# Regrouping a split-product QKV matmul: pairs of row blocks in groups of two, and a later second half of the leftover columns

## The chip, the cores and the metric

The kernel runs on one core of a Trainium2 chip. The metric is the device time of one execution in microseconds (us). Engines are named as the profile names them: PE is TensorE (matmul), PEld its weight loads, DVE is VectorE, ACT is ScalarE, POOL is GpSimd, SP is SyncE, which issues most of the DMAs; ACTq and SPq are the DMA issues of ACT and SP.

## The reference

```python
def reference(x, w_qkv):            # x: 16 x 512 x 768, w_qkv: 768 x 2304, float32
    qkv = np.matmul(x, w_qkv)       # 8192 x 768 times 768 x 2304
    q, k, v = qkv[..., :768], qkv[..., 768:1536], qkv[..., 1536:]
    return np.stack([q, k, v], axis=0).astype(np.float32)
```

## The kernel before

The 8192 rows of x are taken as 32 **pairs** p = 0 to 31, each of two blocks of 128 rows. K = 768 is six slices of 128 (KT = 6), in two halves of three (KH = 3). Of the 2304 columns, 2048 are two **quads** (q = 0 and 1) of two blocks of 512 columns; the other 256 columns, in the middle, are the remaining columns, `REM`.

A quad of a pair is a 2 x 2 by 2 x 2 block product (row blocks by K halves, K halves by column blocks). It is computed with seven block products in place of eight, in Winograd's form. Each product is three matmuls of 128 x 128 by 128 x 512. Products 1 and 2 use rounded copies of x and w in bf16 (`xb`, `b1`). Products 3 to 7 use sums of blocks in fp32r: of x in `s` (made by `sums_x`, five operations on POOL, L211 to L215), of w in `t` (made once by `sum_w`, L120 on DVE) and in `b22`. The remaining columns are plain bf16 products: `rem`, twelve matmuls with 256 columns for a pair (L299).

The order of work is written out by hand (`manual_schedule`): each engine does its instructions in the order in which the program issues them. A pair in the steady part is `two(a, b, early)`, with a and b its quads:

1. product 1 of a and of b (bf16); ACT copies each result to the output tile `o` (`evacuate`, L253).
2. `early()`: the work ahead for pair p+1 and the loads for pair p+2. `ahead(p+1)` is `transpose` (L154, one DVE instruction), `round_x` (L191, a cast to bf16 on POOL) and `sums_x` on POOL. The load of a pair (`load_x`) is four DMAs, two from SP and two from ACT.
3. `rem(p)`, and ACT's copy of it (L316) and its store (L317).
4. product 2 of a and of b (bf16); DVE adds each to `o` (L266).
5. products 6, 6, 5, 7, 5, 7, 4, 3, 4, 3 of a and b (fp32r), with copies by ACT (L269, L275, L279) and additions by DVE (L276, L282); a quad is stored after its product 3 (`store_quad`, two DMAs on SP).

So PE changes from fp32r to bf16 and back once for each pair. The pools hold 8 PSUM banks (`ps`), 5 output tiles (`o`), 3 `xin`, 2 `xf`, 4 `xb` and 2 `s`. A single further buffer, `both`, holds at first a staged block of w and its bf16 copy `bt`, and then the output tile of quad 1 of pair 2.

Pairs 0 to 2 run while w is still being loaded. Pairs 0 and 1 are done as plain bf16 products by K slices: `block(0, 0, ...)`, the first 512 columns, and `block(0, 1, bt, ...)`, the second 512 (L472), whose w slices are cast by DVE and ACT as they land (`cast_j`, L448 and L450). Then come, in this order on PE: the remaining columns of pairs 0 and 1 (`rems_by_halves`, L327, 24 matmuls: K half 0 of both pairs, then K half 1), products 1 and 2 of the first quad of pair 2, `rem(2)`, products 5 and 6 of that quad, and so on. `w_rem[0]` and `w_rem[1]`, the two K halves of the remaining columns of w, are loaded and cast to bf16 by one DMA each from POOL's queue (L435). `hold(src)` puts a one-column copy to a tile `mark` on POOL (L430) ahead of them, so that POOL waits there until `src` has landed: here the last slice of the first 512 columns.

For pair 2, DVE turns the rows in two halves (`transpose(2, 2)`), and ACT rounds one row block at a time (`round_row`, L200). On DVE the first half stands behind `sum_w(0, 2)`, which needs the last slice of the second 512 columns.

Of the kernel before, what the change touches and what calls it, by code (L numbers as in the profile page):

```python
# [10 lines left out]
def kernel(  # L11
# [130 lines left out]
    def load_x(p, other):  # L142
        xin[p] = xin_pool.tile([P, 2 * P // G, KC], fp32, name="xin")
        load_x_half(p, 0, nc.sync)
        if other is not None:
            load_x_half(p, 1, other)

    def transpose(p, parts=1):
        t = xf_pool.tile([P, KT, 2 * P], fp32, name="xf")
        turned = t[:].rearrange("p j (g b) -> p g j b", b=G)  # L150
        rows = xin.pop(p)[:].rearrange("p g (a j) -> p g j a", a=G)
        n = 2 * P // G // parts
        for g in range(0, 2 * P // G, n):
            nc.vector.transpose(turned[:, g:g + n], rows[:, g:g + n])  # L154
        xf[p] = t

# [27 lines left out]
            [xb[p][:, n, r * P:(r + 1) * P] for n in ks], [t[:] for t in ps]  # L186
        )

    def round_x(p):
        xb[p] = xb_pool.tile([P, KT, 2 * P], bf16, name="xb", tag="xb")  # L190
        nc.gpsimd.tensor_copy(out=xb[p][:], in_=xf[p][:])  # L191

    act, dve = nc.scalar, nc.vector

    def round_row(p, r, eng):
        n = slice(r * P, (r + 1) * P)
        if r == 0:
            xb[p] = xb_pool.tile([P, KT, 2 * P], bf16, name="xb", tag="xb")
        if eng is act:
            eng.activation(xb[p][:, :, n], xf[p][:, :, n], ident)  # L200
        else:
            eng.tensor_copy(out=xb[p][:, :, n], in_=xf[p][:, :, n])

    def sums_x(p, eng=None):
        t = xf.pop(p)
        a11, a12 = t[:, :KH, :P], t[:, KH:, :P]
        a21, a22 = t[:, :KH, P:], t[:, KH:, P:]
        s = s_pool.tile([P, 5, KH, P], f32r, name="s")
        sr[p] = s
        sums = {  # L210
            1: lambda g: g.tensor_tensor(s[:, 1], a21, a22, op=add),  # L211
            2: lambda g: g.tensor_tensor(s[:, 2], s[:, 1], a11, op=sub),  # L212
            3: lambda g: g.tensor_tensor(s[:, 3], a11, a21, op=sub),  # L213
            0: lambda g: g.tensor_copy(out=s[:, 0], in_=a22),
            4: lambda g: g.tensor_tensor(s[:, 4], a12, s[:, 2], op=sub),  # L215
        }
        if eng is not None:
            return sums
        for n in (1, 2, 3, 0, 4):
            sums[n](nc.gpsimd)  # L220
# [5 lines left out]
    def quad(p, q, pool=o_pool, tag="o"):  # L226
        u = Quad()
        u.p, u.q = p, q
        u.o = pool.tile([P, 2, 2 * CB], fp32, name="o", tag=tag)
        u.x = u.y = u.z = None  # L230
        return u
# [20 lines left out]
    def evacuate(u):  # L252
        nc.scalar.activation(u.o[:, 0, :CB], u.x[:], ident)  # L253

    def do(u, n, out=True):
        c11, c12 = u.o[:, 0, :CB], u.o[:, 0, CB:]
        c21, c22 = u.o[:, 1, :CB], u.o[:, 1, CB:]
        if n == 1:
            u.x = bank()
            product(u, 1, u.x, True)  # L260
            if out:
                evacuate(u)
        elif n == 2:
            u.z = bank()
            product(u, 2, u.z, True)
            nc.vector.tensor_tensor(c11, c11, u.z[:], op=add)  # L266
        elif n == 6:
            product(u, 6, u.x, False)
            nc.scalar.activation(c12, u.x[:], ident)  # L269
        elif n == 5:  # L270
            u.y = bank()
            product(u, 5, u.y, True)
        elif n == 7:
            product(u, 7, u.x, False)
            nc.scalar.activation(c22, u.x[:], ident)  # L275
            nc.vector.tensor_tensor(c22, c22, u.y[:], op=add)  # L276
        elif n == 4:
            product(u, 4, u.x, False)
            nc.scalar.activation(c21, u.x[:], ident)  # L279
        elif n == 3:  # L280
            product(u, 3, u.y, False)
            nc.vector.tensor_tensor(c12, c12, u.y[:], op=add)  # L282
# [21 lines left out]
    def rem(p, eng=nc.sync, between=None):  # L304
        ps = ps_pool.tile([P, 2, REM], fp32, name="ps")
        rem_row(p, 0, ps[:, 0, :])
        if between is not None:
            between()
        rem_row(p, 1, ps[:, 1, :])
        return rem_copied(p, ps, eng)  # L310

    def rem_copied(p, ps, eng=nc.sync):

        def copied():
            o = or_pool.tile([P, 2, REM], fp32, name="orem")
            act.activation(o[:], ps[:], ident)  # L316
            return lambda: eng.dma_start(rows_of(1, p, R_OFF - H, R_OFF - H + REM), o[:])  # L317

        return copied

    def rems_by_halves(pairs):
        banks = [ps_pool.tile([P, 2, REM], fp32, name="ps") for _ in pairs]
        for h in range(2):
            for p, ps in zip(pairs, banks):
                for r in range(2):
                    for j in range(KH):
                        nc.tensor.matmul(  # L327
                            ps[:, r, :], xb[p][:, h * KH + j, r * P:(r + 1) * P],
                            w_rem[h][:, j, :], start=(h == 0 and r == 0 and j == 0),
                            stop=(h == 1 and j == KH - 1), skip_group_check=True,  # L330
                        )
        return [rem_copied(p, ps) for p, ps in zip(pairs, banks)]

    def two(a, b, early, u=None):

        do(a, 1)
        do(b, 1, u is None)
        if u is None:
            early()
            rem(a.p)()()  # L340
        else:
            middle(u)
            copied = rem(a.p, between=lambda: third(u))
            evacuate(b)
            early()
            copied()()
            fourth(u)
        do(a, 2)
        do(b, 2)
        do(a, 6)  # L350
        do(b, 6)
        do(a, 5)
        do(a, 7)
        do(b, 5)
        do(b, 7)
        do(a, 4)
        do(a, 3)
        store_quad(a)
        do(b, 4)
        do(b, 3)  # L360
        store_quad(b)
# [14 lines left out]
    def last(a, b):  # L376

        p = a.p

        def rem_stored(r):  # L380
            ps = bank()
            rem_row(p, r, ps[:, :REM])
            o = or_pool.tile([P, 2, REM], fp32, name="orem")
            nc.scalar.activation(o[:, 0, :], ps[:, :REM], ident)  # L384
            row = (2 * p + r) * P
            nc.scalar.dma_start(out_flat[1, row:row + P, R_OFF - H:R_OFF - H + REM], o[:, 0, :])  # L386

        do(a, 1)
        do(b, 1)
        do(a, 2)  # L390
        do(a, 6)
        do(b, 2)
        do(b, 6)
        for u in (a, b):
            store_cols(u, 0, 0, CB, nc.sync)
        for u in (a, b):
            do(u, 5)
            do(u, 7)
            store_cols(u, 1, CB, 2 * CB, nc.sync)
        do(a, 4)  # L400
        store_cols(a, 1, 0, CB, nc.scalar)
        rem_stored(0)
        do(b, 4)
        store_cols(b, 1, 0, CB, nc.scalar)
        for u in (a, b):
            do(u, 3)
            store_cols(u, 0, CB, 2 * CB, nc.sync)
        rem_stored(1)
# [19 lines left out]
    def hold(src):  # L428
        mark = m_pool.tile([P, 1], fp32, name="mark")
        nc.gpsimd.tensor_copy(out=mark[:], in_=src)  # L430

    hold(stage[0, 1, 0][:, KH - 1, :1])
    for h in range(2):
        rows = w_qkv.rearrange("(p j) n -> p j n", j=KT)[:, h * KH:(h + 1) * KH]
        nc.gpsimd.dma_start(w_rem[h][:], rows[:, :, R_OFF:R_OFF + REM])  # L435
    hold(xin[2][:, 0, :1])
# [65 lines left out]
    def ahead(p):  # L502
        transpose(p)
        round_x(p)
        sums_x(p)
# [28 lines left out]
    for f in late0:  # L534
# [5 lines left out]
    sum_w(0, 2)  # L540
    nc.gpsimd.tensor_copy(out=b22[0][:], in_=stage[0, 1, 1])
    late = block(
        0, 1, bt, [((j, ), range(4)) for j in range(KH)] + [(range(KH, KT), range(4))]
    )
    rems = rems_by_halves(range(2))
    transpose(2, 2)

    late[0]()
    late[1]()
    round_row(2, 0, act)  # L550
    rem_stores = [rems[0]()]
    late[2]()
    late[3]()
    round_row(2, 1, act)
    rem_stores.append(rems[1]())
    load_blocks(1, 1)
    for store in rem_stores:
        store()
# [7 lines left out]
    sums[2](dve)  # L566
    sum_w(0, 3)
    sums[3](dve)
    sums[4](dve)

    u = quad(2, 0)
    do(u, 1)
    do(u, 2)
    cast_j(1, 0, b1[1], 0)
    rem2 = rem(2)
    middle(u, (5, 6))
# [38 lines left out]
    do(u2, 1)  # L615
    do(u2, 2)

    for p in range(ND + 1, NP):
        def early():
            if p + 1 < NP:  # L620
                ahead(p + 1)
            if p + 2 < NP:
                load_x(p + 2, nc.sync if p <= ND + 2 else nc.scalar)

        a, b = quad(p, 0), quad(p, 1)
        if p == ND + 1:
            two(a, b, early, u2)
        elif p < NP - 1:
            two(a, b, early)
        else:  # L630
            last(a, b)


# [28 lines left out]
```

## Time and profile before

| what | value |
|---|---|
| time, median of 3 runs | 360.31 us (359.99 to 360.98) |
| the profiled execution: time | 361.83 us |
| the profiled execution: span of its instructions | 360.0 us |
| PE busy | 353.4 us (98%), 1780 matmuls |
| DVE, ACT, POOL busy | 227.8, 185.6, 178.6 us |
| granted TensorE clock | 1.0 |
| DMA | 107.73 MB, mean 299 GB/s |
| DMA share and rate, 20.5 to 55.3 us | 1.01, 344 GB/s |
| DMA share and rate, 55.3 to 345 us | 0.92, 294 GB/s |

A PE that is busy is not a PE at its peak: a matmul's record overlaps the next one's, so what counts is the distance between starts. "Idle before" in a row is the engine's idle time ahead of it, with what ended it behind the arrow.

### The profile page before, as it was taken

The page shows a single profiled execution, that of the slowest core. Times are in us where ns is not written, and L with a number is a line of the kernel's source. Part 1 is how long each engine was busy: PE and PEld are TensorE (multiplying, and loading weights), DVE is VectorE, ACT ScalarE, POOL GpSimd, SP SyncE. Part 2 cuts the span into 40 slices and gives each one's busy share as a digit, 9 for nine tenths or more (in the row PEclk, how much of TensorE's full clock was granted, in tenths as well). Part 3 has the DMA queues.
Part 4 walks back from the last instruction along what each step waited for, and adds up shares of the span by engine and source line. Part 5 has one row for each costly group of instructions (what it writes and reads, how often), then busy time and mean ns, then how long its engine had stood idle before and what let it go on. Part 6 is the DMA issues. An engine that isn't in the chain of part 4 may idle for free.

```text
span 360.0 us, 5279 instructions
## 1 busy us (share of the span) xinstructions
PE 353.4 (98%) x1780; PEld 251.2 (70%) x1780; DVE 227.8 (63%) x244; ACT 185.6 (52%) x316; POOL 178.6 (50%) x187
## 2 busy tenths in 40 slices
PE   7999999999999999999999999999999999999995
PEld 3465577777777777777777777777777777777764
DVE  2789776756566675566675566675556676556643
ACT  4469744545454545454545444455444445545443
POOL 0221676446664445664445665444665444665420
PEclk9999999999999999999999999999999999999999
DMA  7998999898998999899999899998999998989767
GB/s 271 330 356 306 332 359 394 257 321 308 275 325 300 296 275 291 280 322 301 291 283 286 284 310 308 292 283 285 288 297 315 293 294 272 296 283 322 292 238 257
DMA packets 82107, 107.73 MB, mean 299 GB/s; under 512 B 5409, under 2 KB 62241, under 8 KB 82081
## 3 DMA queue, kind: packets, MB, share of 16 engines
q1 hardware_dynamic: 66672, 96.35, 82.4%
q10 hardware_dynamic: 14608, 10.65, 8.9%
q0 software_dynamic: 800, 0.39, 0.8%
q8 instruction: 14, 0.23, 0.3%
q14 instruction: 13, 0.10, 0.1%
HBM read 32.28 MB, written 75.50 MB: 299 GB/s over the span
## 4 chain that ended last, share of the span: by engine, by line
PE 93%; DMA 5%; ACT 1%; ACTq 1%; issue 0%
PE ps L244 78%; PE ps L299 11%; PE ps L472 4%; DMA st<-in_w_qkv_dram 3%; DMA touch<-in_x_dram 1%; PE ps L327 1%; ACT o L279 0%; ACTq L370 0%; ACT orem L384 0%; ACT both L448 0%; ACTq L416 0%; ACTq L386 0%; ACTq L384 0%
## 5 line engine op out<-in xcount | busy, mean ns | idle before, releaser
L244 PE MATMUL ps<-t,s 128*128 128x512 f32 x720 | 181.1, 399 | 0.0
L244 PEld LDWEIGHTS ps<-t,s 128*128 128x128 f32 x720 | 134.9, 188 | 30.9 <-ACT o L269 0.3
L191 POOL CAST xb<-xf 128x1536 bf16<-128x1536 f32 x28 | 40.9, 1462 | 131.1 <-DVE xf L154 131.1
L276 DVE TENSOR_TENSOR o<-o,ps 128x512 f32<-128x512 f32 x58 | 39.9, 687 | 90.5 <-ACT o L275 90.5
L154 DVE STREAM_TRANSPOSE xf<-xin 128x1536 f32<-128x1536 f32 (+1 forms) x32 | 88.9, 2783 | 2.6 <-DMA xin<-in_x_dram 2.5
L244 PE MATMUL ps<-b,xb 128*128 128x512 bf16 x360 | 87.7, 380 | 0.0
L244 PEld LDWEIGHTS <-xb 128*128 128x128 bf16 x360 | 32.8, 98 | 37.3 <-issue 7.6
L269 ACT ACTIVATE o<-ps 128x512 f32<-128x512 f32 x60 | 35.9, 598 | 44.0 <-PE ps L244 41.3
L275 ACT ACTIVATE o<-ps 128x512 f32<-128x512 f32 x58 | 34.7, 598 | 44.3 <-PE ps L244 44.3
L282 DVE TENSOR_TENSOR o<-o,ps 128x512 f32<-128x512 f32 x60 | 41.2, 687 | 21.4 <-PE ps L244 20.2
L244 PE MATMUL ps<-b,s 128*128 128x512 f32 x180 | 50.4, 389 | 0.0
L253 ACT ACTIVATE o<-ps 128x512 f32<-128x512 f32 x60 | 35.8, 597 | 24.4 <-DVE o L282 20.6
L279 ACT ACTIVATE o<-ps 128x512 f32<-128x512 f32 x60 | 35.9, 598 | 24.2 <-PE ps L244 21.3
L299 PE MATMUL ps<-w_rem,xb 128*128 128x256 bf16 x360 | 44.6, 273 | 0.0
L299 PEld LDWEIGHTS <-xb 128*128 128x128 bf16 x360 | 34.9, 98 | 11.1 <-issue 1.1
L266 DVE TENSOR_TENSOR o<-o,ps 128x512 f32<-128x512 f32 x60 | 37.8, 670 | 2.0 <-ACT o L253 1.3
L244 PEld LDWEIGHTS ps<-b,s 128*128 128x128 f32 x180 | 33.8, 188 | 7.1
L212 POOL TENSOR_TENSOR s<-s,xf 128x384 fp32r<-128x384 f32 x29 | 29.4, 1014 | 2.3
L215 POOL TENSOR_TENSOR s<-xf,s 128x384 fp32r<-128x384 f32 x29 | 29.4, 1015 | 0.0
L213 POOL TENSOR_TENSOR s<-xf 128x384 fp32r<-128x384 f32 x29 | 29.4, 1013 | 0.0
L211 POOL TENSOR_TENSOR s<-xf 128x384 fp32r<-128x384 f32 x29 | 29.3, 1012 | 0.0
L316 ACT ACTIVATE orem<-ps 128x512 f32<-128x512 f32 x31 | 18.5, 597 | 20.6 <-PE ps L299 20.1
(47 smaller groups left out, 125.9 us busy)
## 6 DMA issues: line engine op xcount, KB each, us to landing
out_dram<-o SPq DMA_DIRECT2D x62, 768.0 KB, 4.9
out_dram<-o SPq DMA_DIRECT2D x65, 256.0 KB, 4.0
xin<-in_x_dram SPq DMA_DIRECT2D x62, 192.0 KB, 6.9
xin<-in_x_dram ACTq DMA_DIRECT2D x50, 192.0 KB, 4.3
out_dram<-orem SPq DMA_DIRECT2D x31, 256.0 KB, 5.9
st<-in_w_qkv_dram SPq DMA_DIRECT2D x11, 256.0 KB, 5.8
st<-in_w_qkv_dram SPq DMA_DIRECT2D x3, 768.0 KB, 8.7
xin<-in_x_dram SPq DMA_DIRECT2D x4, 384.0 KB, 5.1
```

What stands on the lines that cost most here:

```text
L154: nc.vector.transpose(turned[:, g:g + n], rows[:, g:g + n])
L191: nc.gpsimd.tensor_copy(out=xb[p][:], in_=xf[p][:])
L212: 2: lambda g: g.tensor_tensor(s[:, 2], s[:, 1], a11, op=sub),
L244: nc.tensor.matmul(ps[:], lhs[j], rhs[j], start=(start and j == 0), stop=(j == KH - 1), skip_group_check=True,)
L253: nc.scalar.activation(u.o[:, 0, :CB], u.x[:], ident)
L266: nc.vector.tensor_tensor(c11, c11, u.z[:], op=add)
L269: nc.scalar.activation(c12, u.x[:], ident)
L275: nc.scalar.activation(c22, u.x[:], ident)
L276: nc.vector.tensor_tensor(c22, c22, u.y[:], op=add)
L279: nc.scalar.activation(c21, u.x[:], ident)
L282: nc.vector.tensor_tensor(c12, c12, u.y[:], op=add)
L299: nc.tensor.matmul(ps, xb[p][:, j, r * P:(r + 1) * P], w_rem[j // KH][:, j % KH, :], start=(j == 0), stop=(j == KT - 1), skip_group_check= ...
```

## The change

Two parts of the order are changed.

**At the start.** The load of `w_rem[1]` gets a `hold` of its own: POOL now waits for the last slice of the second 512 columns before it issues this DMA. `rems_by_halves` only does K half 0 at once and hands back K half 1, which is done behind products 1 and 2 of pair 2's first quad; these move up. ACT's copies of both pairs' remaining columns, and their stores, follow K half 1. The addition of product 2 (`add_z`) is moved between the sums on DVE. In `block(0, 1, ...)` the fourth K slice is also done for all four tiles before the last two slices are done tile by tile.

**Pairs 6 to 29.** They run as twelve groups of two (`group`): products 1, `rem` and products 2 of the first pair, then the same of the second pair, then the fp32r products of the first pair and then of the second (`rounded`). One output tile of four is taken from the buffer `both`. The transposition of pair p+3 now stands on DVE between the additions of product 2 and those of the first pair's fp32r products; `sums_x` of the second pair begins at the group's start, with `round_x` after its first sum. Loads are issued one or two pairs earlier in pairs 3 to 5, and from SP except for two of the eight DMAs of a group. Pairs 3 to 5, 30 and 31 keep the order of before; pair 5 carries the transposition of pair 7 in two parts (`turns`).

```diff
@@ -145,14 +145,20 @@
         if other is not None:
             load_x_half(p, 1, other)
 
-    def transpose(p, parts=1):
+    def transpose(p, parts=1, split=False):
         t = xf_pool.tile([P, KT, 2 * P], fp32, name="xf")
         turned = t[:].rearrange("p j (g b) -> p g j b", b=G)
         rows = xin.pop(p)[:].rearrange("p g (a j) -> p g j a", a=G)
         n = 2 * P // G // parts
-        for g in range(0, 2 * P // G, n):
-            nc.vector.transpose(turned[:, g:g + n], rows[:, g:g + n])
+        turns = [
+            lambda g=g: nc.vector.transpose(turned[:, g:g + n], rows[:, g:g + n])
+            for g in range(0, 2 * P // G, n)
+        ]
         xf[p] = t
+        if split:
+            return turns
+        for turn in turns:
+            turn()
 
 
 
@@ -186,9 +192,10 @@
             [xb[p][:, n, r * P:(r + 1) * P] for n in ks], [t[:] for t in ps]
         )
 
-    def round_x(p):
+    def round_x(p, t=None):
+        t = xf[p] if t is None else t
         xb[p] = xb_pool.tile([P, KT, 2 * P], bf16, name="xb", tag="xb")
-        nc.gpsimd.tensor_copy(out=xb[p][:], in_=xf[p][:])
+        nc.gpsimd.tensor_copy(out=xb[p][:], in_=t[:])
 
     act, dve = nc.scalar, nc.vector
 
@@ -252,6 +259,10 @@
     def evacuate(u):
         nc.scalar.activation(u.o[:, 0, :CB], u.x[:], ident)
 
+    def add_z(u):
+        c11 = u.o[:, 0, :CB]
+        nc.vector.tensor_tensor(c11, c11, u.z[:], op=add)
+
     def do(u, n, out=True):
         c11, c12 = u.o[:, 0, :CB], u.o[:, 0, CB:]
         c21, c22 = u.o[:, 1, :CB], u.o[:, 1, CB:]
@@ -263,7 +274,8 @@
         elif n == 2:
             u.z = bank()
             product(u, 2, u.z, True)
-            nc.vector.tensor_tensor(c11, c11, u.z[:], op=add)
+            if out:
+                add_z(u)
         elif n == 6:
             product(u, 6, u.x, False)
             nc.scalar.activation(c12, u.x[:], ident)
@@ -320,7 +332,8 @@
 
     def rems_by_halves(pairs):
         banks = [ps_pool.tile([P, 2, REM], fp32, name="ps") for _ in pairs]
-        for h in range(2):
+
+        def half(h):
             for p, ps in zip(pairs, banks):
                 for r in range(2):
                     for j in range(KH):
@@ -329,9 +342,11 @@
                             w_rem[h][:, j, :], start=(h == 0 and r == 0 and j == 0),
                             stop=(h == 1 and j == KH - 1), skip_group_check=True,
                         )
-        return [rem_copied(p, ps) for p, ps in zip(pairs, banks)]
-
-    def two(a, b, early, u=None):
+
+        half(0)
+        return lambda: half(1), [rem_copied(p, ps) for p, ps in zip(pairs, banks)]
+
+    def two(a, b, early, u=None, turns=()):
 
         do(a, 1)
         do(b, 1, u is None)
@@ -347,12 +362,20 @@
             fourth(u)
         do(a, 2)
         do(b, 2)
+        rounded(a, b, turns)
+
+    def rounded(a, b, turns=()):
+
+        for t in turns[:1]:
+            t()
         do(a, 6)
         do(b, 6)
         do(a, 5)
         do(a, 7)
         do(b, 5)
         do(b, 7)
+        for t in turns[1:]:
+            t()
         do(a, 4)
         do(a, 3)
         store_quad(a)
@@ -429,8 +452,8 @@
         mark = m_pool.tile([P, 1], fp32, name="mark")
         nc.gpsimd.tensor_copy(out=mark[:], in_=src)
 
-    hold(stage[0, 1, 0][:, KH - 1, :1])
     for h in range(2):
+        hold(stage[0, 1, h][:, KH - 1, :1])
         rows = w_qkv.rearrange("(p j) n -> p j n", j=KT)[:, h * KH:(h + 1) * KH]
         nc.gpsimd.dma_start(w_rem[h][:], rows[:, :, R_OFF:R_OFF + REM])
     hold(xin[2][:, 0, :1])
@@ -540,19 +563,23 @@
     sum_w(0, 2)
     nc.gpsimd.tensor_copy(out=b22[0][:], in_=stage[0, 1, 1])
     late = block(
-        0, 1, bt, [((j, ), range(4)) for j in range(KH)] + [(range(KH, KT), range(4))]
+        0, 1, bt,
+        [((j, ), range(4)) for j in range(KH + 1)] + [(range(KH + 1, KT), range(4))],
     )
-    rems = rems_by_halves(range(2))
+    second_half, rems = rems_by_halves(range(2))
     transpose(2, 2)
 
     late[0]()
     late[1]()
     round_row(2, 0, act)
-    rem_stores = [rems[0]()]
     late[2]()
     late[3]()
+    u = quad(2, 0)
+    do(u, 1)
+    do(u, 2, False)
     round_row(2, 1, act)
-    rem_stores.append(rems[1]())
+    second_half()
+    rem_stores = [r() for r in rems]
     load_blocks(1, 1)
     for store in rem_stores:
         store()
@@ -566,11 +593,9 @@
     sums[2](dve)
     sum_w(0, 3)
     sums[3](dve)
+    add_z(u)
     sums[4](dve)
 
-    u = quad(2, 0)
-    do(u, 1)
-    do(u, 2)
     cast_j(1, 0, b1[1], 0)
     rem2 = rem(2)
     middle(u, (5, 6))
@@ -615,20 +640,55 @@
     do(u2, 1)
     do(u2, 2)
 
-    for p in range(ND + 1, NP):
+    def group(p):
+
+        quads = [quad(p, 0, bt_pool, "both"), quad(p, 1)]
+        do(quads[0], 1)
+        do(quads[1], 1)
+        turned = xf[p + 1]
+        sums = sums_x(p + 1, nc.gpsimd)
+        sums[1](nc.gpsimd)
+        round_x(p + 1, turned)
+        for n in (2, 3, 0, 4):
+            sums[n](nc.gpsimd)
+        transpose(p + 2)
+        round_x(p + 2)
+        if p + 4 < NP:
+            load_x(p + 4, nc.sync)
+        rem(p)()()
+        do(quads[0], 2)
+        do(quads[1], 2)
+        quads += [quad(p + 1, q) for q in range(2)]
+        do(quads[2], 1)
+        do(quads[3], 1)
+        if p + 5 < NP:
+            load_x(p + 5, nc.scalar)
+        rem(p + 1)()()
+        do(quads[2], 2)
+        do(quads[3], 2)
+        if p + 2 < NE:
+            transpose(p + 3)
+        rounded(*quads[:2])
+        sums_x(p + 2)
+        rounded(*quads[2:])
+
+    NG, NE = ND + 4, NP - 2
+    extra = {NG - 3: (NG, ), NG - 1: (NG + 3, )}
+    for p in range(ND + 1, NG):
+        late_turns = []
+
         def early():
-            if p + 1 < NP:
-                ahead(p + 1)
-            if p + 2 < NP:
-                load_x(p + 2, nc.sync if p <= ND + 2 else nc.scalar)
-
-        a, b = quad(p, 0), quad(p, 1)
-        if p == ND + 1:
-            two(a, b, early, u2)
-        elif p < NP - 1:
-            two(a, b, early)
-        else:
-            last(a, b)
+            ahead(p + 1)
+            for n in (p + 2 + (p > NG - 3), ) + extra.get(p, ()):
+                load_x(n, nc.sync)
+            if p == NG - 1:
+                late_turns.extend(transpose(NG + 1, 2, True))
+
+        two(quad(p, 0), quad(p, 1), early, u2 if p == ND + 1 else None, late_turns)
+    for p in range(NG, NE, 2):
+        group(p)
+    two(quad(NE, 0), quad(NE, 1), lambda: ahead(NE + 1))
+    last(quad(NE + 1, 0), quad(NE + 1, 1))
 
 
 # ---- launch: one core; inputs and outputs as the reference has them ----
```

## The prediction

> **What bounds the kernel now.** I read the page first: busy shares and the chain that ended last.
>
> ```profile
> PE 353.4 (98%) x1780; PEld 251.2 (70%) x1780; DVE 227.8 (63%) x244; ACT 185.6 (52%) x316; POOL 178.6 (50%) x187
> ...
> PE 93%; DMA 5%; ACT 1%; ACTq 1%; issue 0%
> ```
>
> PE carries 93% of the chain, DMA 5%. The chain in order of time shows where: up to 18.4 us it is landings of w and one cast, from there to 352.9 us PE alone. In the steady part it repeats without a gap:
>
> ```profile
> 164.15 1.31 PE ps L299 x12
> 165.46 9.43 PE ps L244 x42
> 174.89 1.31 PE ps L299 x12
> ```
>
> A pair takes 1.31 + 9.43 = 10.74 us. No engine makes PE wait, and the change removes no matmul. So it can gain only where PE loses time between matmuls, or at the start. The timeline of PE gives the spacing of fp32r matmuls inside a run:
>
> ```profile
> 157.69 3.11 PE L244 MATMUL ps<-t,s 128*128 128x512 f32 x13
> 160.63 0.61 PE L244 MATMUL ps<-b,s 128*128 128x512 f32 x2
> ```
>
> 13 starts in 160.63 - 157.69 = 2.94 us: 0.226 us each. The start, from the timelines of PE, POOL and DVE:
>
> ```profile
> 14.97 3.19 PE L472 MATMUL ps<-both,xb 128*128 128x512 bf16 x14
> 18.39 2.32 PE L472 MATMUL ps<-both,xb 128*128 128x512 bf16 x10 [0.23 <-ACT both L448]
> 20.54 2.78 PE L327 MATMUL ps<-w_rem,xb 128*128 128x256 bf16 x24
> 23.16 1.46 PE L244 MATMUL ps<-b,xb 128*128 128x512 bf16 x6
> ```
>
> ```profile
> 12.80 0.44 POOL L430 COPY mark<-st 128x1 f32<-128x1 f32 x1 [11.49 <-DMA st<-in_w_qkv_dram]
> 13.18 1.69 POOL L435 DMA_DIRECT2D w_rem<-in_w_qkv_dram  x2
> ```
>
> ```profile
> 17.81 1.76 DVE L120 TENSOR_TENSOR t<-st,t 128x1536 fp32r<-128x1536 f32 x1 [0.66 <-DMA st<-in_w_qkv_dram]
> 19.66 1.60 DVE L154 STREAM_TRANSPOSE xf<-xin 128x768 f32<-128x768 f32 x1
> ```
>
> See in them the one wait of PE (for the cast of the last w slice, which ACT starts at 17.70), the 24 remaining-column matmuls that follow, and pair 2's rows being turned on DVE beneath them. The rows of the tile w_rem add:
>
> ```profile
> DMA to landing us min/median/max: 6.5/7.0/7.6
> ```
>
> The issues are 13.18 and 14.10, so the halves landed at 19.7 and 21.7.
>
> **The groups (pairs 6 to 29).** Spacings: bf16 with 512 columns (23.16 to 24.46)/6 = 0.217; with 256 columns (20.54 to 23.16)/24 = 0.109. A pair's sum is 30 x 0.226 + 12 x 0.217 + 12 x 0.109 = 6.78 + 2.60 + 1.31 = 10.69. The period is 10.74, so 0.04 to 0.05 us a pair goes at the change from fp32r to bf16 and back. A group makes this change once instead of twice: 12 x 0.04 = -0.5 us. That is all this part can give.
>
> What must still be hidden, counted from a group's start:
> - xb of the second pair. POOL does one sum (1.01) and the cast (1.46) after the last product of the group before: ready at 2.5 to 2.8. PE needs it after 12 + 12 bf16 matmuls, at 3.9. Over a second of cover.
> - The second transposition (L154, 2.94) now stands between DVE's additions of product 2 and of product 7. Before, in the pair at 155 us, the last L266 ended at 156.85, L276 ran from 159.43 to 160.12, and product 3 of the same quad started at 160.63. Now DVE ends the transposition at 159.80 and the addition at 160.48. It fits with 0.15 to spare, the tightest cover in the group.
> - The output tile in `both`: stored 14.1 after the start, landing takes 4 to 9 us, wanted again at 22. ACT then copies late at worst, and PE does not need that copy before 7.8 us into the next group.
> - Queues: SP issues 16 DMAs a group where it issued 14 in two pairs (0.4 to 1.2 us each, in 21.4), ACT 2 instead of 4. Pairs 3 to 5 load up to two pairs more: 2 x 0.79 MB at the 344 GB/s of that stage is 4.6 us of DMA spread over 30. Stores queue behind these loads, but five output tiles give each about six us. I cost these at nothing.
>
> **The start.**
> - The fourth K slice over all tiles: 14 matmuls from 14.97 would end at 18.0, PE starts at 18.39. Now 17 matmuls stand ahead of the last slice, to 18.65: no wait. -0.39; the block ends at 20.15.
> - Twelve remaining-column matmuls: to 21.46. Then products 1 and 2 of pair 2, which need row block 0 of xb. Its chain is untouched: last slice, L120, L154, ACT's L200 from 21.29 to 22.13. Before, 24 matmuls hid it to 23.16; half of that cover is gone. PE waits about 0.75, to 22.2, and is done with products 1 and 2 at 23.5.
> - K half 1 now wants `w_rem[1]`. POOL's new copy starts 0.05 after its slice landed, at 17.73 (as 12.80 follows a cast at 12.77), takes 0.18 (the row of the other mark, at 19.68), and the DMA is issued at 17.9. How long it takes is not shown for this place. The second DMA landed only 2.0 after the first, and the DMA view has no packet of POOL's queue until 15.3, 2.1 after the issue: at least 4.1, landing 22.0. The slowest row, 7.6, would be 25.5. I take 6.5, the first DMA's: same size, nothing before it in its queue, SP's loads beside it all the time. Landing 24.4, PE at 24.45, a further wait of 0.95.
> - Then 12 + 12 matmuls (K half 1, `rem(2)`) of 0.109: 27.07. Before, `rem(2)` ended at 24.46 + 1.31 = 25.77. The start loses 1.30. From there to the end PE had no wait, so nothing gives it back.
> - Behind it: ACT's copies of the remaining columns come about a us later, and the first cast of block(1, 0) after them, near 27.3; PE wants it at 28.4. SP's two stores hold the loads of pair 3 up by about 1 us; those wait for slots until 32 anyway, and DVE turns pair 3 at 35.86.
>
> The Trainium skill, "DMA: Bandwidth & Descriptors", section "Anatomy of one DMA — SWDGE (gpsimd) path", gives 2.0 us plus bytes over 436 GB/s. For the 393 KB read here that is an estimate of 2.9 us, a landing at 20.8 and a total of 360.2. The row of 6.5 disagrees, and I go by the row.
>
> **Sum.** +1.30 - 0.5 = +0.8 us. The profiled execution took 361.83 (span 360.0), 1.5 above the median; on its scale the forecast is 362.6, on the median's 360.31 + 0.8 = **361.1 us**.
>
> **The rivals.**
> 1. `w_rem[1]` is in time (landed by 23.5; the 2.0 between the two landings speaks for it). Only the wait for xb stays: 23.5 + 2.62 = 26.12, +0.35 - 0.5: 360.2.
> 2. The slices land sooner as well. From 14.72 to 17.70 three slices took 1 us each, where those before took 0.65; POOL's DMAs ran beside them. With half of that traffic gone, L120 could start 0.7 earlier, as DVE idled 0.66 before it, and neither wait is left: -0.39 - 0.5: 359.4. Against it: the first half landed at 19.7, so what ran beside the slices was mostly that half, which stays.
> 3. Slower: POOL is held by DVE. At 39.03 a POOL cast of 768 elements took 3.87 us, where 1536 take 1.46; DVE ran two L120 sums beside it, from 38.81 to 42.21. The new mark and its DMA fall on the L120 of 17.81. If they wait for its end at 19.57, `w_rem[1]` lands at 26.1, `rem(2)` ends at 28.7, +2.95 - 0.5: 362.8. It decides if POOL's copy starts after 17.81 instead of at 17.73, or if the issue itself is held. Against it: the issues at 13.18 and 14.10 took 0.92 and 0.78 beside DVE's casts of 13.38 and 14.03. The Trainium skill, "SBUF — State Buffer", section "Who interferes with whom", has whoever starts first hold the shared ports for a whole instruction, and infers that a two-input DVE sum does not stop descriptor writing. By that rule the start order alone decides, and 17.73 keeps the forecast.
> 4. The groups stall: if the second transposition ends 0.3 later than worked out, product 3 waits 0.15 in each of 12 groups: 1.8, with the rest as forecast 362.9. DVE's 28 transpositions lie at 2.94 to 3.04, against it.
> 5. The 0.04 is not from the change of type: no gain from the groups, 361.6.
>
> **How the numbers follow.** A measurement of this kernel can tell about 0.3%, 1.1 us, from no change: 359.2 to 361.4. Forecast (360.5 to 361.7) 0.34, rival 1 0.18, rival 2 0.20, rival 3 0.14, rival 4 0.09, rival 5 0.05. Slower: rivals 3, 4 and 5 and the upper part of the forecast, 0.28 + 0.09 = 0.37. Faster: half of rival 2, 0.10; nothing in the trace gives more than 0.9. The same: 0.53. The range from 359.3 to 362.8 leaves out the lower part of rival 2 (0.07) and about half of rivals 3 and 4 (0.12).
>
> **What would show it.** Right: a group of 21.44 us in the chain; no wait at the last slice; PE waiting for ACT's L200 rounding near 21.5 and for the DMA of w_rem near 23.5; the L435 issue near 17.9. Wrong: no wait for w_rem (rival 1 or 2), a mark on POOL that ends near 19.6 (3), PE waiting for DVE's addition ahead of product 3 (4), a period of 21.48 (5).

## The result and the profile after

| | before | after |
|---|---|---|
| median of 7 runs | 360.31 us (359.97 to 361.00) | 363.25 us (361.85 to 365.12) |
| ratio, 95% interval | | 1.0078 (1.0057 to 1.0100) |
| profiled execution: time, span | 361.83, 360.0 us | 365.12, 363.3 us |

The changed kernel is slower by 2.9 us. The prediction said 361.1 us and a range to 362.8: it was wrong, on the slow side.

The page of the changed kernel, busy time and shares of the chain: PE is busy as before, and DMA has grown from 5% to 7% of the chain.

```profile
PE 353.2 (97%) x1760; PEld 253.0 (70%) x1780; DVE 230.4 (63%) x245; ACT 185.6 (51%) x316; POOL 177.1 (49%) x188
...
PE 91%; DMA 7%; ACTq 1%; ACT 1%; issue 0%; POOL 0%
```

Its chain in order of time (start, us, what) names the new piece: the DMA of the second half of the remaining columns. Farther down it shows a group, 21.44 us from the two products of 104.74 to those of 126.18.

```profile
16.64 8.59 DMA w_rem<-in_w_qkv_dram
25.27 1.66 PE ps L340 x12
26.93 2.56 PE ps L311 x12
...
104.74 2.59 PE ps L251 x12
107.33 1.31 PE ps L311 x12
108.64 14.92 PE ps L251 x66
126.18 2.59 PE ps L251 x12
```

The timeline of PE at the start (L495 was L472, L340 was L327, L251 was L244, L311 was L299):

```profile
13.91 5.34 PE L495 MATMUL ps<-both,xb 128*128 128x512 bf16 x24
19.09 1.47 PE L340 MATMUL ps<-w_rem,xb 128*128 128x256 bf16 x12
21.18 1.47 PE L251 MATMUL ps<-b,xb 128*128 128x512 bf16 x5 [0.62 <-ACT xb L207]
25.27 1.66 PE L340 MATMUL ps<-w_rem,xb 128*128 128x256 bf16 x12 [2.62 <-DMA w_rem<-in_w_qkv_dram]
26.72 2.77 PE L311 MATMUL ps<-w_rem,xb 128*128 128x256 bf16 x12
```

The wait at the last slice is gone. Two new ones stand in the brackets, 0.62 us for xb and 2.62 us for `w_rem[1]`. The last two rows hold something else: the same twelve matmuls that took 1.31 us take up to 2.6 in the chain. Windows of all engines (stretch, its length, then busy time and count for PE, PEld, DVE, ACT and POOL, then the granted clock, the DMA share and GB/s) show why:

```profile
21.18:25.27 4.09, 1.42 (x5) 0.60 (x7) 3.95 (x6) 2.19 (x4) 0.87 (x1) 1.00 1.12 359
25.27:27.00 1.73, 1.73 (x14) 1.44 (x14) 1.73 (x3) 0.63 (x2) 0.00 (x0) 0.83 1.05 407
27.00:28.00 1.00, 1.00 (x6) 0.70 (x5) 1.00 (x1) 1.00 (x2) 0.00 (x0) 0.50 1.03 395
30.00:31.00 1.00, 1.00 (x6) 0.63 (x5) 0.00 (x0) 0.00 (x0) 1.00 (x1) 1.00 0.77 218
```

After the wait the granted clock is 0.50; the trace has it so from 26.42 for 3.41 us. Two of the seven executions (365.12 and 365.06, mean clock 0.995) are of this kind; the other five have a mean clock of 0.999 or 1.0, and their median is 362.82.

An account of the profiled executions, by the first matmul of `block(0, 1, ...)` and the first product of pair 4 in the timelines of PE:

| | before | after |
|---|---|---|
| block(0, 1) starts | 14.97 | 13.91 |
| pair 4's product 1 | 55.28 | 59.04 |
| between the two | 40.31 | 45.13 |
| from there to the last run of remaining columns | 300.13 | 299.65 |

The start is longer by 4.82: -0.39 at the last slice, +0.78 for xb, +2.79 for `w_rem[1]` (by starts, so a little over the idle time in the brackets), and a remainder of 1.64, which fits the half clock (3.41 us at half speed do 1.7 us less work). The rest is shorter by 0.48. That this block began 1.06 us later before is part of that one execution: in the traces of the experiments it begins at 13.55 to 14.41.

### The profile page after: what moved, and what is told of

Same layout as the page of the kernel before. It is cut to its first block, busy times and chain, and to the rows that moved or that the text cites. A ratio compares the mean times of both kernels' runs of the same rounds, so it can differ in the third digit from the quotient of the medians.

```text
span 363.3 us, 5212 instructions
## 1 busy us (share of the span) xinstructions
PE 353.2 (97%) x1760; PEld 253.0 (70%) x1780; DVE 230.4 (63%) x245; ACT 185.6 (51%) x316; POOL 177.1 (49%) x188
## 4 chain that ended last, share of the span: by engine, by line
PE 91%; DMA 7%; ACTq 1%; ACT 1%; issue 0%; POOL 0%
PE ps L251 77%; PE ps L311 11%; DMA st<-in_w_qkv_dram 3%; PE ps L495 3%; DMA w_rem<-in_w_qkv_dram 2%; DMA touch<-in_x_dram 1%; PE ps L340 0%; ACT o L291 0%; ACTq L393 0%; ACT orem L407 0%; ACTq L439 0%; ACTq L409 0%; POOL mark L453 0%; ACTq L407 0%
## 5 line engine op out<-in xcount | busy, mean ns | idle before, releaser
L251 PE MATMUL ps<-t,s 128*128 128x512 f32 x720 | 178.8, 396 | 0.0
L251 PEld LDWEIGHTS ps<-t,s 128*128 128x128 f32 x720 | 135.2, 188 | 29.9 <-ACT o L281 0.3
L154 DVE STREAM_TRANSPOSE xf<-xin 128x1536 f32<-128x1536 f32 (+1 forms) x33 | 91.0, 2763 | 0.3 <-DMA xin<-in_x_dram 0.3
L218 POOL TENSOR_TENSOR s<-xf 128x384 fp32r<-128x384 f32 x29 | 30.8, 1061 | 116.5 <-PE ps L251 115.1
L251 PE MATMUL ps<-b,xb 128*128 128x512 bf16 x342 | 82.0, 379 | 1.8 <-ACT xb L207 0.6
L251 PEld LDWEIGHTS <-xb 128*128 128x128 bf16 x360 | 33.7, 98 | 37.8 <-issue 4.7
L251 PE MATMUL ps<-b,s 128*128 128x512 f32 x180 | 50.4, 389 | 0.0
L311 PE MATMUL ps<-w_rem,xb 128*128 128x256 bf16 x360 | 45.9, 278 | 0.0
L311 PEld LDWEIGHTS <-xb 128*128 128x128 bf16 x360 | 35.5, 100 | 11.4 <-issue 1.1
L251 PEld LDWEIGHTS ps<-b,s 128*128 128x128 f32 x180 | 33.8, 188 | 7.1
L220 POOL TENSOR_TENSOR s<-xf 128x384 fp32r<-128x384 f32 x29 | 29.3, 1009 | 0.0
```

Of the source, the lines that this page charges most:

```text
L154: lambda g=g: nc.vector.transpose(turned[:, g:g + n], rows[:, g:g + n])
L251: nc.tensor.matmul(ps[:], lhs[j], rhs[j], start=(start and j == 0), stop=(j == KH - 1), skip_group_check=True,)
L311: nc.tensor.matmul(ps, xb[p][:, j, r * P:(r + 1) * P], w_rem[j // KH][:, j % KH, :], start=(j == 0), stop=(j == KT - 1), skip_group_check= ...
```

## The experiments

### One part of the change alone

The first kernel has the start of before and the groups of the changed kernel (label e2_groups_only):

```diff
-    for h in range(2):
-        hold(stage[0, 1, h][:, KH - 1, :1])
+    hold(stage[0, 1, 0][:, KH - 1, :1])
+    for h in range(2):
...
-        [((j, ), range(4)) for j in range(KH + 1)] + [(range(KH + 1, KT), range(4))],
+        [((j, ), range(4)) for j in range(KH)] + [(range(KH, KT), range(4))],
...
+    second_half()                  # behind K half 0, products 1 and 2 again after the sums
```

> Start as before the change, pairs 3 to 31 as changed (groups, loads from SP, split transposition). Theory: a group is 21.44 us where two pairs were 21.48, no stall: 12 x 0.04 = 0.48 less than before, 359.8, ratio 0.9987. Rival (loads moved ahead and stores in bursts hold something up in pairs 3 to 5 or at the end): at or above 360.3.

Measured: 360.31 us against 360.48 before, ratio 0.9997 (0.9989 to 1.0006). The median fell by 0.17 us, not by the 0.48 expected, and 360.31 lies where the rival put it; its trace, below, shows the 0.4 to 0.5 all the same. The other kernel has the start of the changed kernel and the steady loop of before (label e4_start_only):

```diff
-    for p in range(NG, NE, 2):
-        group(p)
+    for p in range(ND + 1, NP):
+        ...                        # two(a, b, early), as before
```

> Start as changed, pairs 3 to 31 as before the change. Theory: all of the loss is in the start, so it is 0.48 us slower than the changed kernel: 363.7 by medians (362.3 to 365.6 as its start varies). Rival (the groups cost something): as fast as the changed kernel or faster.

Measured: 364.30 us, ratio 1.0110 (1.0093 to 1.0127). Its trace has the second load landing 9.16 us after the issue:

```profile
PE ps L340 <- DMA w_rem<-in_w_qkv_dram: 3.5, 1, 3.5
```

So all of the loss is the start's. In the traces, from pair 4's first product to the last run of remaining columns the kernels with the old loop take 300.13 and 300.14 us (before, this one), those with groups 299.65, 299.73 and, below, 299.75 twice. There the groups give 0.4 to 0.5, as worked out, and nothing holds them up. The medians don't show it: the interval above reaches from 0.4 us faster to 0.2 slower.

The kernel with the groups alone shows one more thing. It has the old order of slices, and yet its block runs its 24 matmuls without a break:

```profile
14.41 5.34 PE L495 MATMUL ps<-both,xb 128*128 128x512 bf16 x24
19.59 2.78 PE L340 MATMUL ps<-w_rem,xb 128*128 128x256 bf16 x24
```

The wait at the last slice, which the change was to take away, stands in the profiled execution of before, 1.5 us above its median, and not in this one, the only other trace with the old order.

### The load issued earlier

The changed kernel with one `hold` ahead of both loads, as before (label e1_early_load):

```diff
-    for h in range(2):
-        hold(stage[0, 1, h][:, KH - 1, :1])
+    hold(stage[0, 1, 0][:, KH - 1, :1])
+    for h in range(2):
```

> The changed kernel, but POOL issues the load of w_rem[1] right behind that of w_rem[0], as before the change; the order on PE and all the rest stay as changed. Theory (the whole loss is the late landing of w_rem[1]: PE's wait of 2.8 us for it, and the clock that is halved for 3.4 us after it): no wait for w_rem, a clock of 1.0, and only the wait of 0.78 us for row block 0 of pair 2 is left: 360.31 - 0.39 + 0.78 - 0.48 = about 360.2. Rival (the moved products, copies and stores cost by themselves): it stays above 361.5.

Measured: 360.66 us, ratio 1.0005 (0.9996 to 1.0014), 0.45 above the time expected, about the 0.39 of the last slice that was counted there. The wait for `w_rem[1]` is gone (issue 12.92, landing 20.29), the one for xb stays:

```profile
18.73 1.47 PE L340 MATMUL ps<-w_rem,xb 128*128 128x256 bf16 x12
21.11 1.47 PE L251 MATMUL ps<-b,xb 128*128 128x512 bf16 x6 [0.91 <-ACT xb L207]
```

That one line of the change costs 2.6 us by the two medians, 2.8 if each is taken against its own runs of before. Nor does the later load bring the slices sooner: the last three land at 14.15, 14.87 and 16.31 here, at 14.26, 15.04 and 16.47 in the changed kernel.

Next, the second load held on the fourth K slice in place of the sixth (label e7_hold_earlier):

```diff
-        hold(stage[0, 1, h][:, KH - 1, :1])
+        hold(stage[0, 1, h][:, KH - 1 if h == 0 else 0, :1])
```

> The changed kernel with the second half's load held on the fourth K slice instead of the last one: issue near 14.4 instead of 16.6. Theory, the lateness of the issue alone costs the 2.7 us: it lands 7.2 to 7.6 us after the issue (as in the kernel with both loads early), at 21.6 to 22.0, PE needs it at 22.7, and the wait for it is gone; the wait for xb of 0.6 to 0.9 stays. Time 360.2 to 360.7, ratio 0.9995 to 1.001. Rival, any load held behind slices takes 8.6 us and lands beside SyncE's blocks: landing near 23.0 to 23.6, a wait of 0.3 to 0.9, time 360.8 to 361.6.

Measured: 360.64 us, ratio 1.0004 (0.9996 to 1.0013), a time as the theory had it, but not by its steps. The issue came at 15.60, not at 14.4, and still the landing was early, 4.55 us after it, at 20.14. The timeline of POOL, and the landings of both halves in the rows of the tile:

```profile
14.20 1.46 POOL L453 COPY mark<-st 128x1 f32<-128x1 f32 x1 [1.30 <-DMA st<-in_w_qkv_dram]
15.60 0.78 POOL L458 DMA_DIRECT2D w_rem<-in_w_qkv_dram  x1
```

```profile
DMA to landing us min/median/max: 4.5/5.4/6.2
```

Only 1.04 us between this issue and that of the changed kernel (16.64) move the landing by 5.1 us (20.14, 25.23). SyncE's first block load was issued at 16.35 here and at 16.84 there. So neither theory had the size. It looks as if not the time of the issue counts, but what is queued beside it; the next experiment tests that.

### What makes the landing slow

SyncE's four block loads, 3.1 MB, follow the last slice on its queue too. Here they are held until `w_rem[1]` has landed (label e5_blocks_held):

```diff
+    wait = m_pool.tile([1, 16], bf16, name="wait")
+    nc.sync.dma_start(wait[:], w_rem[1][:1, 0, :16])
     load_blocks(1, 0)
```

> The changed kernel with SyncE's four block loads (3.1 MB, the next ones in its queue) held until the second half of the remaining columns has landed. Theory, competition: the 8.6 us are some 3 us until the first packet and then a transfer that shares the 16 DMA engines with these loads. Without them the 393 KB should land 4.9 to 5.5 us after the issue, near 21.5 to 22.2, and PE should not wait for them. Rival, a slow path of POOL's queue in itself: 8 us or more again, landing near 25. The time of the whole kernel isn't meant to be better: the blocks come about 5 us later, and block(1, 0) will wait for them.

The landing came 4.50 us after the issue of 16.77, at 21.27, and K half 1 followed the products at once. SyncE's small load, which waits for that landing, starts right behind it, ahead of the blocks:

```profile
21.29 0.61 SPq L461 DMA_DIRECT2D wait<-w_rem  x1
```

```profile
21.40 1.47 PE L251 MATMUL ps<-b,xb 128*128 128x512 bf16 x5 [0.55 <-ACT xb L207]
22.70 1.47 PE L340 MATMUL ps<-w_rem,xb 128*128 128x256 bf16 x12
```

Competition it is. The packets of POOL's queue show each part of it growing (the time of 363.43 us is that of blocks that come late, and tells nothing here):

| second load, us after its issue | changed kernel | blocks held |
|---|---|---|
| first packet | 2.96 | 1.61 |
| 90% of its packets done | 6.05 | 3.40 |
| last packet | 8.30 | 4.22 |
| landed | 8.59 | 4.50 |

The other suspect was DVE's two-input sum, which starts at 16.59 beside the issue. It is moved behind the transposition (label e6_sum_later):

```diff
-    sum_w(0, 2)
...
     transpose(2, 2)
+    sum_w(0, 2)
```

> The changed kernel with DVE's two-input sum sum_w(0, 2) moved behind the transposition of pair 2, so that no two-input sum runs beside the second DMA issue of POOL. Theory, DVE delays the writing of descriptors: the first packet of that DMA then comes about 2.2 us after the issue instead of 3.1, and it lands about 0.9 us sooner (some 7.7 us). Rival, DVE has no part in it: first packet again 3.1 us after the issue, landing 8.2 to 9.2 us after it, PE's wait again 2.6 or more.

First packet 3.4 us after the issue, landing 9.25, PE's wait 3.25: the delay is there without the sum, so DVE has no part in it. This and the kernel with the blocks held are single executions. This one took 365.85 us, with half clock from 25.51 for 3.41 us.

### What the wait costs beside its length

The changed kernel with 14 matmuls on zeros between product 2 and K half 1, so that PE is busy through most of the wait (label e3_fill_wait):

```diff
+    busy(14)
     second_half()
```

> The changed kernel with 14 matmuls on a zero tile (512 columns, 3.0 us) put on PE between products 1 and 2 of pair 2 and K half 1 of the remaining columns, that is, in PE's wait for w_rem[1]; their result is used by nothing. Theory (the idle PE of 2.8 us is what lets the granted clock fall to half, at a cost of 1.7 us): the clock stays 1.0 in all executions, the landing is no earlier, and the slow executions of the changed kernel (365.1) are gone: 361.9 to 363.4 with a smaller spread. Rival (the clock falls for another reason): clock below 1.0 in some executions, up to 365.

Measured: 364.01 us (363.42 to 364.37), ratio 1.0093 (1.0078 to 1.0107), above the range expected, for the most part because the zeros ended 0.7 us after the landing of 25.15. The clock stayed at 1.0 in the start, and the twelve matmuls take their 1.31 us again:

```profile
22.83 3.19 PE L466 MATMUL ps<-zero 128*128 128x512 bf16 x14
25.85 1.47 PE L340 MATMUL ps<-w_rem,xb 128*128 128x256 bf16 x12
27.16 1.47 PE L311 MATMUL ps<-w_rem,xb 128*128 128x256 bf16 x12
```

None of its four executions has a mean clock under 0.999. Four are few against two of seven; but of the 69 executions of the six kernels, above and below, whose profiled execution has no wait of 1 us at this place, none has a mean clock under 0.997 either. The other way round, with the late load and all 24 matmuls ahead of the products, PE idles in one piece (label e10_late_24):

```diff
     second_half, rems = rems_by_halves(range(2))
+    second_half()
...
-    second_half()
```

> The changed kernel with its late load, but all 24 remaining-column matmuls ahead of pair 2's products, as before. Theory, the landing of the second half (8 to 9 us after an issue near 16.6, at 24.6 to 25.8) sets the start and the products merely hid 1.3 us of it and gained nothing for xb: after the landing 12 + 6 products + 12 matmuls follow instead of 12 + 12, so 1.3 us more than the changed kernel: 364.5 (363.8 to 365.5), PE's wait for w_rem 4.2 to 5.4, none for xb. Rival, the 2.6 us of wait come from the order of PE, not from the load: 360.5 to 362, a wait under 2.

Measured: 366.33 us (363.14 to 367.33), ratio 1.0126 (1.0086 to 1.0166): above what was expected, as the clock was not in it. Windows of the profiled execution (columns as above) and its waits:

```profile
20.85:24.02 3.17, 0.01 (x1) 0.00 (x0) 3.03 (x4) 1.60 (x3) 0.87 (x1) 1.00 1.15 325
24.02:30.85 6.83, 6.00 (x23) 3.26 (x23) 2.27 (x4) 1.96 (x4) 0.77 (x1) 0.50 0.64 246
```

```profile
PE ps L340 <- DMA w_rem<-in_w_qkv_dram: 4.0, 1, 4.0
```

A wait of 4.0 us brings half clock for 6.83 us, twice 3.41. Three of its four executions have a mean clock of 0.990 to 0.994 and take 366.08 to 367.33 us; the fourth, at 0.998, takes 363.14.

### Versions without the waits

Early load and all 24 matmuls ahead of the products, with the rest as changed (label e8_all_covered):

```diff
+    hold(stage[0, 1, 0][:, KH - 1, :1])
     for h in range(2):
-        hold(stage[0, 1, h][:, KH - 1, :1])
...
     second_half, rems = rems_by_halves(range(2))
+    second_half()
...
-    second_half()
```

> Both loads of the remaining columns early and all 24 of their matmuls ahead of pair 2's products, as before; the block with the fourth slice over all tiles, and the groups, as changed. Theory: it keeps what the change gives (no wait at the last slice, -0.39; groups, -0.48) and drops both of its waits (xb 0.75, w_rem 2.8): 359.4 to 359.7, ratio 0.9975 to 0.9985, and below the kernel with both loads early but only twelve matmuls ahead of the products (1.0005) by about 0.75 us. Rival: the start's small waits move from run to run with the landings and nothing of the -0.39 is kept: 360.0, ratio 0.999 to 1.0.

Measured: 360.33 us against 360.55, ratio 0.9995 (0.9986 to 1.0004). The sum of -0.87 didn't come; the ratio is the rival's. The waits it was to drop are gone, the 0.39 was not there to be had, and the start lost 0.3 in a new place:

```profile
21.69 1.46 PE L251 MATMUL ps<-b,xb 128*128 128x512 bf16 x5
22.98 1.76 PE L311 MATMUL ps<-w_rem,xb 128*128 128x256 bf16 x12
```

`rem(2)` takes 1.76 where it took 1.47: after its six matmuls of row block 0 it waits for row block 1 of xb, whose rounding (ACT, 23.03 to 23.86) stands behind ACT's copy of product 1. With the second load held on the third K slice instead, and the 24 matmuls ahead as in the last kernel (label e9_hold_third, its `hold` against the changed kernel):

```diff
-        hold(stage[0, 1, h][:, KH - 1, :1])
+        hold(stage[0, 1 - h, h][:, KH - 1, :1])
```

> As the kernel with everything covered (24 remaining-column matmuls ahead of the products, fourth slice over all tiles, groups), but with the second load held on the third K slice: issue near 13.7, between the early place (13.0) and the place of the earlier hold (15.6), ahead of SyncE's block loads. Theory, order against SyncE's loads decides: it lands 4.5 to 6.5 us after its issue, at 18.3 to 20.2, before PE wants it at 20.4; pair 2's second rows, which land at 20.75 with the early load, land sooner (19.5 to 20.3), so that product 5 loses its 0.3 us. Time 359.9 to 360.3, ratio 0.9985 to 0.9995. Rival, the sums behind the rows decide nothing: 360.3, ratio 0.9995 again.

Measured: 360.63 us, ratio 1.0005 (0.9996 to 1.0014): no gain. The issue of 14.08 landed 6.70 later, at 20.77, and PE waited 0.18 us for it; pair 2's last rows landed at 21.18, no sooner than 20.75, so the expectation was wrong in that step and the 0.3 stayed. The last version has the start of before, with the fourth slice over all tiles, and the groups (label e11_groups_slice, its edit against the kernel with the groups alone):

```diff
-        [((j, ), range(4)) for j in range(KH)] + [(range(KH, KT), range(4))],
+        [((j, ), range(4)) for j in range(KH + 1)] + [(range(KH + 1, KT), range(4))],
```

> The kernel of before with two parts of the change: the groups, and the fourth K slice over all tiles. Early load, 24 matmuls ahead of the products, and ACT's rounding of row block 1 ahead of its copy of product 1, as before. Theory, only the groups' 0.40 us is real, since the wait at the last slice is not there in most executions: from the block's first matmul to pair 4's product 1 39.9 us, as in the kernel with the groups alone, and no wait of 0.3 inside rem(2), which the kernel with everything covered had: 360.1 to 360.3 where before is 360.5, ratio 0.9985 to 0.9995. Rival, the wait at the last slice is regular and adds its 0.39: 359.7 to 359.9, ratio 0.9975 to 0.9983.

Measured: 360.02 us (359.74 to 361.53) against 360.37, ratio 0.9993 (0.9983 to 1.0003). From the block's first matmul to pair 4's first product it takes 39.95 us, with the groups alone 39.90: in these two executions the order of the slices gives nothing. It is the lowest median of all the kernels here, but its interval holds 1: a gain of 0.35 us would fit what the traces give the groups, and is not shown.

## Why the prediction was wrong

**The step that failed** is the landing of `w_rem[1]`. The prediction took 6.5 us, the row of the first half, "same size, nothing before it in its queue, SP's loads beside it all the time". It was 8.59, and 7.9 to 9.3 in the four other kernels that kept the late issue with the blocks beside it. That is beyond the 7.6 which the prediction held for the slowest end. The three likenesses were true and the fourth was missing: the first half shares the DMA engines with slices and rows of 96 to 256 KB, the second with four loads of 768 KB that are issued within two us of it. SyncE's queue in the changed kernel:

```profile
16.84 0.43 SPq L93 DMA_DIRECT2D both<-in_w_qkv_dram  x1
17.31 2.16 SPq L93 DMA_DIRECT2D st<-in_w_qkv_dram  x3
```

This order was in the trace of before, where the same loads, issued at 18.05 to 19.59, follow the last slice:

```profile
18.05 0.43 SPq L93 DMA_DIRECT2D both<-in_w_qkv_dram  x1
18.53 1.79 SPq L93 DMA_DIRECT2D st<-in_w_qkv_dram  x3
```

But the prediction tied the new issue only to the slice. With the blocks held the landing takes 4.50. In the profiled execution the wait came to 2.79 us instead of 0.95: +1.84, which alone takes 361.1 to 362.9.

**Missing altogether** was the clock. An idle PE was priced at its length; behind 2.62 us of it the clock was 0.50 for 3.41 us, another 1.64 in the profiled execution and in two of seven. It moves the median from 362.82 to 363.25. The Trainium skill, "TensorE: Matmul & The Clock Gate", section "Part 1: The HAM clock gate (the "warmup" mystery)", gives a free-running window of 3413 ns and half clock after an idle window: the lengths of 3.41 and 6.83 agree.

The clock's record in the traces agrees with a window that runs on by itself, too: the fall comes 20.48 us after the record's first entry, from which on it gives full clock, in three kernels (5.94 to 26.42 in the changed one) and 17.07 in the fourth, 6 and 5 times 3.413, while that first entry lies anywhere from 3.9 to 7.0 us. A whole window without work was not needed: in the 3.41 us ahead of the fall PE stood still for 2.3 (changed kernel), 2.9, 3.0 and 3.2 us. If the wait of 2.6 us falls across the end of a window, less of it lies in each, which would explain why it costs the clock in some executions only. That is argued: no trace is kept of an execution of the changed kernel at full clock.

**The slices, -0.39.** Right for the profiled execution (no wait after), mis-sized for the median, where it is probably near 0: the other trace with the old order doesn't have the wait. The prediction had noted that this execution lay 1.5 us above the median and didn't ask which of its waits that was.

**Right were** the wait for xb (0.75 predicted, 0.78); the mark and the issue (2.93 us after the block's start predicted, 2.73 found); the groups (-0.5; -0.48 in the trace, 21.44 us a group); and the covers counted for the groups, since PE has no wait in them. The waits are those of the profiled execution: 0.78 + 2.79, less 0.48, give +3.1, but the five executions at full clock lie 2.5 above before, so theirs were probably shorter by some 0.6 us in all (an estimate from these numbers). That the median's +2.9 comes near 3.1 is luck: two executions at half clock raise it.

**The rivals.** Rival 1 (`w_rem[1]` in time) and rival 2 (slices sooner) are refuted by the landings. Rival 3 came closest with its 362.8, by a cause that was not at work: POOL was not held, as its timeline and DVE's show.

```profile
16.52 0.18 POOL L453 COPY mark<-st 128x1 f32<-128x1 f32 x1 [3.51 <-DMA st<-in_w_qkv_dram]
16.64 0.78 POOL L458 DMA_DIRECT2D w_rem<-in_w_qkv_dram  x1
```

```profile
16.59 1.76 DVE L120 TENSOR_TENSOR t<-st,t 128x1536 fp32r<-128x1536 f32 x1 [0.53 <-DMA st<-in_w_qkv_dram]
```

The mark starts 0.07 ahead of the sum and takes 0.18; the DMA is issued beside it. Its mechanism does exist: with the earlier hold the mark started at 14.20, 0.34 behind a sum of 13.86 to 15.61, and took 1.46. The prediction's rule that the start order decides (the Trainium skill, "SBUF — State Buffer", section "Who interferes with whom") agrees with both rows. Rivals 4 and 5 are refuted by the period of 21.44 and by PE's waits.

The estimate that the prediction made from the Trainium skill, "DMA: Bandwidth & Descriptors", section "Anatomy of one DMA — SWDGE (gpsimd) path", 2.9 us, is nearer to the 4.50 with the blocks held than to the 8.59 beside them. It prices one transfer by itself; the same page's section "Queues, rings and completion order", by which a DMA engine takes packets of its queues in turn, is the one that bears on this case, and the two landings agree with it.

## What to carry to other kernels

When a transfer is made to wait for another, list what else was waiting for that same moment: here the load was tied to the slice behind which the largest loads of the start are issued, and one us of lead is worth five at the landing. A wait of PE near three us can cost more than its length, so price what follows at half clock as well. And a wait that the profile shows once may be no gain at all when the profiled execution lies above the median, as here by 1.5 us.

## What was not expected of the hardware

- A load of 393 KB from POOL's queue landed 4.5 us after its issue or 9.3, depending on what SyncE had queued beside it; the last tenth of its packets alone took 2.25 us in the changed kernel (0.82 with the blocks held).
- Half clock came in whole pieces of 3.41 us, beginning 3 to 4 us after PE had stopped, by which time PE could be at work again: in the changed kernel PE restarted at 25.27 and the clock fell at 26.42. It came in 2 of 7, 2 of 6 and 3 of 4 executions with waits of 2.6, 3.5 and 4.0 us in the profiled one. The falls lie on a grid of 3.413 us whose position moves from execution to execution. That the place of the wait on this grid decides is argued, not shown.
